# Streaming-encoder layer with a 32-expert MoE on one core: weight streaming in 2 MB buffers with 16 KB pieces

## The chip, the cores and the metric

One core of one Trainium2 chip runs the whole layer, as one program. The metric is the device time in microseconds; a version's time is the median of its runs. Three runs of the kernel before took 1102.35, 1105.44 and 1106.4 us.

## The reference

Input x is 1 x 256 x 1024 in float32. One layer is computed: LayerNorm; a mixer (differential attention with 4 heads beside a gated recurrent branch, both from one 1024 x 2560 projection, then a 1024 x 1024 output projection); a residual LayerNorm; a mixture of experts; a last residual LayerNorm. The mixture is where the bytes are:

```
logits = xt @ w_router + b_router          # 256 tokens, 32 experts
top_v, top_e = lax.top_k(logits, 4);  gates = softmax(top_v)
h = xb @ w_gu[e] + b_gu[e]                 # w_gu[e]: 1024 x 2048
x_glu = minimum(h[..., ::2], 7);  x_lin = clip(h[..., 1::2], -7, 7)
y = (x_glu * sigmoid(1.702 * x_glu) * (x_lin + 1)) @ w_down[e] + b_down[e]   # 1024 x 1024
out = sum over a token's experts of gate * y
```

All weights are float32. An expert has 8 MB of w_gu and 4 MB of w_down, so 32 experts are 384 MB, and every one of them is read once from HBM.

## The kernel before

The mixer comes first. Its weights (w_in in five blocks of 512 columns, w_out in two of 512 rows) and then the experts' weights pass through 1 MB buffers of 8 KB per partition. `wtile` takes one from a pool: pool 0 (`wpool`) has NW1 = 12 buffers in rotation; nine further pools of one buffer each (`wpool2`) are opened only when the mixer's tiles have been given back (L852, ahead of the main loop), in the memory that those tiles had. That makes 21. `SLOTS` says which pool each of 21 successive transfers takes.

`load_chunk` issues the next transfer of `seq`, which lists (expert, h). For h below 8 it is 128 neighbouring rows of w_gu, one row of 8 KB per partition, so a transfer consists of 128 pieces of 8 KB. For h = 8 to 11 it is 256 rows of w_down, two neighbouring rows per partition, also 8 KB. All are issued by SP's queue, in program order. Each transfer takes one of eight completion semaphores in turn and waits until the transfer eight before it has landed; it also waits until TensorE has done the last matmul on the buffer's old content (`reuse_waits="tile"`: on the tile as a whole). `NPRE` = 7 expert transfers are issued while the mixer runs, the other 14 of the first 21 where the nine pools open, and from then on `ahead(e, h)` issues as many as keep the program 21 transfers in front of what expert e has used.

The main loop goes over the experts. `first(e)` runs `gu_mm`: for each of the 8 row blocks k of w_gu four accumulating matmuls per half (two halves b), 64 token slots (CAP) against 512 columns, in the order k = 0 to 5 with both halves, then k = 6 and 7 for each half; then SwiGLU on DVE and ACT. After it come the combine of the pair before, the transposes of the activations (`act_t`), the gather of the next pair's tokens (`gather_mm`) and `down_mm` with the four w_down buffers in four steps. An expert with more than 64 tokens first runs `overflow(e)`, the same work for the surplus, on the same weight buffers. The last two experts' w_gu transfers go ahead of their w_down transfers.

One further transfer group stands in `seq` in front of the w_down of expert LATE = 13: b_down and two LayerNorm rows, three small DMAs into a buffer of the stream, which `start_acc` reads at expert 13.

Features: with one row per partition, row block k holds features 128k to 128k+127. Every operand that is multiplied with w_gu or scaled per feature (`rows_t`, `gather_ps`, `gb1`, the router weights `wr`) has that order.

Of the kernel before, what the change touches and what calls it, by code (L numbers as in the profile page):

```python
# [9 lines left out]
F32 = mybir.dt.float32  # L10
# [7 lines left out]
P = 128  # L18
D = 1024
T = 256  # L20
NT = T // P
KT = D // P
H = 4
NE = 32
# [6 lines left out]
BIGGEST = 3.4028234663852886e38  # L31
NW1 = 12
NW2 = 7
NW3 = 2
LATE = 13
NPRE = 7
SLOTS = (0, 0, 0, 0, 0, 0, 0, 3, 0, 1, 2, 4, 0, 0, 6, 0, 0, 7, 5, 8, 9)
NH = 12
NOF = (T - CAP) // OCAP
# [10 lines left out]
def trunk(ctx, tc, x, ln0_g, ln0_b, w_in, conv_w, conv_b, w_rg_a, b_rg_a, w_rg_x, b_rg_x,  # L50
# [37 lines left out]
    def wtile(name, pool=0):  # L88
        return (wpool, *wpool2)[pool].tile([P, 2048], F32, tag=f"w{pool}", name=name)

    def load_in(c, parts=1, between=()):

        src = w_in[0][:, c * 512:(c + 1) * 512].rearrange("(j p) n -> p j n", p=P)
        ws = []
        for h in range(2):
            w = wtile(f"win{c}_{h}").rearrange("p (j n) -> p j n", j=4)
            n = 4 // parts
            for i in range(0, 4, n):
                SP.dma_start(w[:, i:i + n], src[:, 4 * h + i:4 * h + i + n])
            ws.append(w)  # L100
            for dst, src_s in between if h == 0 else ():
                SP.dma_start(dst, src_s)
        return ws

    def load_out(c):
        ws = []
        for h in range(2):
            w = wtile(f"wout{c}_{h}").rearrange("p (j n) -> p j n", j=2)
            o = c * 512 + h * 256
            SP.dma_start(w, w_out[0][o:o + 256, :].rearrange("(j p) n -> p j n", p=P))  # L110
            ws.append(w)
        return ws
# [47 lines left out]
    wr = pb.tile([P, KT, NE], F32, name="wr")  # L160
    SP.dma_start(wr, w_router[0].rearrange("(j p) e -> p j e", p=P))
    br = pb.tile([1, NE], F32, name="br")
# [12 lines left out]

    seq = [(e, h) for e in range(NE - 2) for h in range(NH)]
    seq += [(NE - 2 + i // KT, i % KT) for i in range(2 * KT)]
    seq += [(e, h) for e in (NE - 2, NE - 1) for h in range(KT, NH)]
    seq.insert(LATE * NH + KT, (LATE, NH))

    def load_chunk():


        i = nchunk[0]
        nchunk[0] += 1
        e, h = seq[i]
        w = wtile(f"we{e}_{h}", SLOTS[i % len(SLOTS)])
        if h < KT:
            SP.dma_start(w, w_gu[0, e][h * P:(h + 1) * P, :])
        elif h == NH:  # L190
            SP.dma_start(w[:NE, :D], b_down[0])
            SP.dma_start(w[NE:NE + 1, :D], ln1_b)
            SP.dma_start(w[:1, D:], ln1_g)
        else:
            s = w_down[0, e].rearrange("(g b p j) n -> p g b (j n)", g=2, p=P, j=2)[:, (h - KT) % 2, (h - KT) // 2]

            for g in (slice(0, D), slice(D, 2 * D)) if i == len(seq) - 1 else (slice(0, 2 * D),):
                SP.dma_start(w[:, g], s[:, g])
        W[e, h] = w

# [53 lines left out]
    def bcast_row(ps, rows, j, start=True, stop=True):  # L254

        PE.matmul(ps, ident[:16, j:j + 1].to_broadcast([16, P]), rows, start=start, stop=stop, skip_group_check=True)

    def small_transpose(dst, src, ps, rows):
# [312 lines left out]
    V.tensor_scalar(gsub, gsub, 1.0 - LAM_INIT, None, op0=OP.mult)  # L571
    small_transpose(gb1.rearrange("p r k -> p (r k)"), rows_1, ps1("gb1_ps"), 16)

# [128 lines left out]
    def rows_t(t, n):  # L702
        ps = ps2(f"rT{t}_{n}")[:, 0] if t == 0 else ps1(f"rT{t}_{n}")
        for j in range(4):
            k = n * 4 + j
            PE.transpose(ps[:, j * P:(j + 1) * P], acc[t][:, k * P:(k + 1) * P], ident)
        return A.activation(rT[:, n * 4:n * 4 + 4, t * P:(t + 1) * P], ps.rearrange("p (j n) -> p j n", j=4), AF.Copy)
# [78 lines left out]
    def gather_ps(S, ps, k, t, start):  # L786
        n = S.shape[-1]
        PE.matmul(ps[:, (k % 4) * n:(k % 4 + 1) * n], n1[t][:, k * P:(k + 1) * P], S[:, t],  # L788
                  start=start, stop=t == NT - 1, skip_group_check=True)
# [61 lines left out]
    sa.close()  # L851
    for i in range(NW2 + NW3):  # L852
        wpool2.append(ctx.enter_context(tc.tile_pool(name=f"wpool{i + 2}", bufs=1, reuse_waits="tile")))
    for _ in range(NW1 - NPRE + NW2 + NW3):
        load_chunk()
    s1p.close()
    pdn = loop.enter_context(tc.tile_pool(name="pdn", bufs=1, space=PSUM, reuse_waits="tile", side="right"))
# [166 lines left out]
    def start_acc(n):  # L1024

        w = W[LATE, NH]
        ns = slice(n * 512, (n + 1) * 512)
# [25 lines left out]
    def ahead(e, h):  # L1053

        while nchunk[0] < min(len(seq), NH * e + h + (e > LATE or (e == LATE and h == NH)) + len(SLOTS)):
            load_chunk()

    def first(e, mid=None):
        gi, gj = where[e]
        ps = gu_mm(e, xgs[gi][1], gj * CAP, CAP, mid)  # L1060
        ahead(e, KT)
        g = gtile(e)
        for b in range(2):
            swiglu(e, ps, b, g)
        return g
# [143 lines left out]
```

## Time and profile before

| | |
|---|---|
| median of three runs | 1105.44 us |
| the profiled execution | 1104.07 us, span 1102.4 us |
| mean granted TensorE clock | 0.974 |
| TensorE busy | 1015.0 us, 92% |
| VectorE / ScalarE / GpSimd busy | 281.0 / 188.6 / 146.6 us |
| read from HBM | 420.52 MB, 382 GB/s over the span |
| w_gu | 256 transfers of 1024 KB, median 20.8 us from issue to landing |
| w_down | 127 of 1024 KB and 2 of 512 KB, median 19.8 us |

The page cuts the span into 40 slices of 27.6 us. TensorE is busy for most of every slice, and so are the DMA engines, so that neither share alone tells which of them the end waits for. That has to be read from what TensorE waits for, stretch by stretch.

### The profile page before, as it was taken

Reading aid. Unit: us, or ns where it says so; the run is one execution under the profiler, and the core shown is the slowest. Engines: PE = TensorE matmul, PEld = TensorE weight load, DVE = VectorE, ACT = ScalarE, POOL = GpSimd, SP = SyncE. Lnnn points to the kernel's source line nnn. Section 1 sums busy time; section 2 is a strip of 40 time slices with the busy share of each in tenths; the row PEclk is TensorE's granted clock in tenths of the full one; section 3 lists DMA queues with packets and bytes.
Section 4 is the critical chain, followed back from the end, with each engine's and each line's share of the span. In section 5 each row is a group of like instructions: output and inputs, shape, how many; then the busy total and the mean of one; then the engine's idle time right before and its main releaser. Section 6 shows DMA issues by size and latency. Waiting matters only on the chain. (4 is left out here: it accounts for less than half of the span.)

```text
span 1102.4 us, 12947 instructions
## 1 busy us (share of the span) xinstructions
PE 1015.0 (92%) x4942; PEld 466.1 (42%) x4942; DVE 281.0 (25%) x625; ACT 188.6 (17%) x426; POOL 146.6 (13%) x221
## 2 busy tenths in 40 slices
PE   8999999999899989888999898988888889999895
PEld 8987644444344433333343333333333434444331
DVE  7978311122022201214211011212111122221023
ACT  5675211111011101110011011110100101111011
POOL 4583202010101010101001010101001001010001
PEclk9999999999999999998899999999999989999998
DMA  8987799999999999989999999999999999999962
GB/s 276 323 335 306 293 393 420 418 419 419 419 419 419 419 419 419 405 352 395 421 419 418 420 410 404 411 393 401 415 389 414 418 391 420 387 410 396 409 272 81
DMA packets 66139, 423.46 MB, mean 384 GB/s; under 512 B 8925, under 2 KB 8990, under 8 KB 16960
## 3 DMA queue, kind: packets, MB, share of 16 engines
q1 hardware_dynamic: 65984, 421.60, 94.5%
q8 instruction: 72, 1.18, 0.4%
q14 instruction: 83, 0.68, 0.2%
HBM read 420.52 MB, written 1.05 MB: 382 GB/s over the span
## 5 line engine op out<-in xcount | busy, mean ns | idle before, releaser
L878 PE MATMUL h<-we,xg 128*64 128x512 f32 (+1 forms) x2112 | 481.8, 610 | 58.9 <-DMA we<-in_w_gu_dram 44.6
L878 PEld LDWEIGHTS h<-we,xg 128*64 128x64 f32 (+1 forms) x2112 | 160.8, 138 | 375.6 <-issue 306.4
L911 PE MATMUL y<-we,actT 128*64 128x512 f32 x1024 | 228.9, 599 | 0.1
L888 DVE TENSOR_SCALAR g<-h 128x256 f32<-128x256 f32 x65 | 27.6, 425 | 694.6 <-PE h L878 694.6
L926 POOL TENSOR_SCALAR sgate<-iota,posm,gate 128x64 f32<-128x64 f32 x96 | 54.1, 582 | 814.9 <-PE gt_ps L934 813.9
L889 ACT ACTIVATE sg<-g 128x256 f32<-128x256 f32 x65 | 27.0, 416 | 596.6 <-DVE g L888 596.6
L911 PEld LDWEIGHTS y<-we,actT 128*64 128x64 f32 x1024 | 71.3, 137 | 135.1 <-issue 128.6
L788 PE MATMUL xg_ps<-S,n 128*128 128x128 f32 (+1 forms) x544 | 67.4, 278 | 0.0
L788 PEld LDWEIGHTS xg_ps<-S,n 128*128 128x128 f32 x544 | 66.3, 195 | 2.6 <-issue 1.6
L940 PE MATMUL cb<-ysb,gtT 128*128 128x512 f32 x116 | 57.5, 618 | 0.0
L1103 ACT ACTIVATE ysb<-y 128x512 f32<-128x512 f32 x30 | 16.3, 595 | 139.2 <-PE y L911 139.2
L942 DVE TENSOR_TENSOR acc<-acc,cb 128x512 f32<-128x512 f32 x58 | 39.5, 681 | 0.0
L385 PE MATMUL pj<-xo,hi 128*128 128x256 f32 x128 | 37.0, 289 | 1.0 <-DVE xo L340 1.0
L796 DVE TENSOR_SCALAR xg<-xg_ps,gb 128x128 f32<-128x128 f32 (+1 forms) x68 | 22.8, 398 | 59.1 <-PE xg_ps L788 59.1
L385 PE MATMUL pj<-xh,hi 128*128 128x256 f32 x128 | 37.2, 291 | 0.2 <-ACT xh L334 0.2
L899 PE MATMUL actT_ps<-ident,g 128*128 128x128 f32 x130 | 29.9, 312 | 7.3 <-DVE g L892 6.3
L385 PE MATMUL pj<-xh,lo 128*128 128x256 f32 x128 | 36.4, 284 | 0.0
L940 PEld LDWEIGHTS cb<-ysb,gtT 128*128 128x128 f32 x116 | 19.6, 189 | 37.9 <-ACT sg L889 21.1
L252 POOL TENSOR_TENSOR lo<-win,hi 128x1024 fp32r<-128x1024 f32 x11 | 32.7, 2993 | 13.0 <-PE pj L385 12.9
L899 PEld LDWEIGHTS actT_ps<-ident,g 128*128 128x128 f32 x130 | 21.6, 202 | 25.0 <-DVE g L892 12.3
L798 ACT ACTIVATE xg<-xg_ps,gb 128x128 f32<-128x128 f32 (+1 forms) x68 | 25.3, 452 | 31.8 <-PE xg_ps L788 31.8
L670 PE MATMUL h<-bgu,pick 128*128 128x512 f32 x64 | 30.5, 479 | 0.0
(271 smaller groups left out, 701.1 us busy)
## 6 DMA issues: line engine op xcount, KB each, us to landing
we<-in_w_gu_dram SPq DMA_DIRECT2D x256, 1024.0 KB, 20.8
we<-in_w_down_dram SPq DMA_DIRECT2D x127, 1024.0 KB, 19.8
win<-in_w_in_dram SPq DMA_DIRECT2D x8, 1024.0 KB, 10.9
wout<-in_w_out_dram SPq DMA_DIRECT2D x4, 1024.0 KB
win<-in_w_in_dram SPq DMA_DIRECT2D x4, 512.0 KB, 8.9
x<-in_x_dram SPq DMA_DIRECT2D x4, 256.0 KB, 3.1
we<-in_w_down_dram SPq DMA_DIRECT2D x2, 512.0 KB
out_dram<-acc SPq DMA_DIRECT2D x4, 256.0 KB, 2.3
```

The lines of the kernel that those rows point to most:

```text
L252: return (eng or V).tensor_sub(lo, src, f32(hi))
L385: PE.matmul(ps[m // 2][:, m % 2], a, b, start=k == 0 and m % 2 == 0 and i == 0, stop=k == KT - 1 and i == 2, skip_group_check=True)
L670: PE.matmul(ps[b], picks[e].rearrange("p g w -> p (g w)"), bgs[b], start=True, stop=False, skip_group_check=True)
L788: PE.matmul(ps[:, (k % 4) * n:(k % 4 + 1) * n], n1[t][:, k * P:(k + 1) * P], S[:, t], start=start, stop=t == NT - 1, skip_group_check=True)
L878: PE.matmul(ps[b][g * w:(g + 1) * w], xg[k // 4][:, k % 4, o:o + w], W[e, k][:, c0:c0 + 512], start=False, stop=k == KT - 1, skip_group_ch ...
L888: V.tensor_scalar(g[:, ns], ps[b][:, 0::2], 7.0, None, op0=OP.min)
L889: A.activation(s, g[:, ns], AF.Sigmoid, scale=1.702)
L899: PE.transpose(ps[:, j * P:(j + 1) * P], gj[:, j], ident)
L911: PE.matmul(ps[n][gs], at[:, 2 * b + j, g * CAP:(g + 1) * CAP], w_dn(e, 2 * g + b, j, n * 512, 512), start=c + j == 0, stop=c + j == 4, sk ...
L926: G.tensor_scalar(sg[:, t, i * CAP:(i + 1) * CAP], iota2[:, 0], posm[:, t, o:o + 1], gate[:, t, o:o + 1], op0=OP.is_equal, op1=OP.mult)
L940: PE.matmul(pp, gt[:, n, t * P:(t + 1) * P], y, start=True, stop=True)
L942: V.tensor_add(acc[t][:, ns], acc[t][:, ns], pp)
```

## The change

Buffers become 2 MB, 16 KB per partition: six in pool 0 and four pools of one, ten in all, plus one 1 MB buffer `bd` that holds b_down and the two rows for good. A w_gu transfer is 256 neighbouring rows, two per partition, as 128 pieces of 16 KB; four of them make an expert. A w_down buffer is filled by two transfers of 1 MB, whose pieces stay 8 KB. w_in and w_out keep their 1 MB transfers, two of which now share a buffer. The three small DMAs move from expert 13 to the place where the pools open. Features are paired to match (feature 2p + j of a 256 block in partition p, row block j), so transposes and gathers read every second column, `gb1` is built by four small matmuls in the place of one, and `wr` is loaded in pieces of 256 bytes where it was 128.

```diff
-NW1 = 12
-NW2 = 7
-NW3 = 2
+NW1 = 6
-NPRE = 7
-SLOTS = (0, 0, 0, 0, 0, 0, 0, 3, 0, 1, 2, 4, 0, 0, 6, 0, 0, 7, 5, 8, 9)
-NH = 12
+NPRE = 4
+SLOTS = (0, 0, 0, 0, 2, 1, 0, 4, 0, 5)
+NH = 6
+NU = 4
...
-        return (wpool, *wpool2)[pool].tile([P, 2048], F32, tag=f"w{pool}", name=name)
+        return (wpool, *wpool2)[pool].tile([P, 4096], F32, tag=f"w{pool}", name=name)
...
-    seq.insert(LATE * NH + KT, (LATE, NH))
...
-        if h < KT:
-            SP.dma_start(w, w_gu[0, e][h * P:(h + 1) * P, :])
-        elif h == NH:
-            SP.dma_start(w[:NE, :D], b_down[0])
-            SP.dma_start(w[NE:NE + 1, :D], ln1_b)
-            SP.dma_start(w[:1, D:], ln1_g)
...
+        if h < NU:
+            SP.dma_start(w, w_gu[0, e].rearrange("(d p j) n -> p d (j n)", p=P, j=2)[:, h])
+            for j in range(2):
+                W[e, 2 * h + j] = w[:, j * 2 * D:(j + 1) * 2 * D]
+            return
+        for g in range(2):
+            s = w_down[0, e].rearrange("(g b p j) n -> p g b (j n)", g=2, p=P, j=2)[:, g, h - NU]
+            c = KT + 2 * (h - NU) + g
+            W[e, c] = w[:, g * 2 * D:(g + 1) * 2 * D]
...
+                SP.dma_start(W[e, c][:, q], s[:, q])
...
+    def pairs(ap):
+
+        return ap.rearrange("p (d q j) -> p d j q", q=P, j=2)
...
-            PE.transpose(ps[:, j * P:(j + 1) * P], acc[t][:, k * P:(k + 1) * P], ident)
+            PE.transpose(ps[:, j * P:(j + 1) * P], pairs(acc[t])[:, k // 2, k % 2], ident)
...
-        PE.matmul(ps[:, (k % 4) * n:(k % 4 + 1) * n], n1[t][:, k * P:(k + 1) * P], S[:, t],
+        PE.matmul(ps[:, (k % 4) * n:(k % 4 + 1) * n], pairs(n1[t])[:, k // 2, k % 2], S[:, t],
...
-    for _ in range(NW1 - NPRE + NW2 + NW3):
+        if i == 2:
+            bd = wpool2[2].tile([P, 2 * D], F32, name="bd")
+    for _ in range(len(SLOTS) - NPRE):
         load_chunk()
+    SP.dma_start(bd[:NE, :D], b_down[0])
+    SP.dma_start(bd[NE:NE + 1, :D], ln1_b)
+    SP.dma_start(bd[:1, D:], ln1_g)
...
-        while nchunk[0] < min(len(seq), NH * e + h + (e > LATE or (e == LATE and h == NH)) + len(SLOTS)):
+        while nchunk[0] < min(len(seq), NH * e + h + len(SLOTS)):
...
-        ahead(e, KT)
+        ahead(e, NU)
```

Where it moves instructions: on SP's queue alone (of the other engines' orders only one copy at expert 13 changes place, and `gb1`'s small matmuls are more). First the queue at the end of the first 20 or 21 MB. `weE_H` is transfer H of expert E; DMAHW0 to DMAHW7 are the eight completion semaphores, the other names are the engines whose use of the memory is waited for. Before, the rows from expert 1's fifth w_gu transfer on:

```order
L189 DMA we1_4_1483<-in_w_gu_dram 128x2048 [waits DMAHW0_49,DVE_49]
L189 DMA we1_5_1485<-in_w_gu_dram 128x2048 [waits DMAHW1_49,PE_49]
L189 DMA we1_6_1487<-in_w_gu_dram 128x2048 [waits DMAHW2_49,PE_49]
L189 DMA we1_7_1489<-in_w_gu_dram 128x2048 [waits DMAHW3_49]
L198 DMA we1_8_1491<-in_w_down_dram 128x2048 [waits DMAHW4_49]
L997 UNCONDITIONAL_BRANCH
L198 DMA we1_9_2528<-in_w_down_dram 128x2048 [waits DMAHW5_49,PE_49]
L198 DMA we1_10_2530<-in_w_down_dram 128x2048 [waits DMAHW6_49,PE_49]
L198 DMA we1_11_2532<-in_w_down_dram 128x2048 [waits DMAHW7_49,PE_49]
L189 DMA we2_0_2534<-in_w_gu_dram 128x2048 [waits DMAHW0_49,PE_49]
```

The same place of the changed kernel:

```order
L189 DMA we1_2_1454<-in_w_gu_dram 128x4096 [waits DMAHW2_49,DVE_49,Pool_49]
L189 DMA we1_3_1456<-in_w_gu_dram 128x4096 [waits DMAHW3_49,PE_49]
L867 DMA bd_1437<-in_b_down_dram 32x1024 [waits DMAHW4_49,PE_49]
L868 DMA bd_1437<-in_ln1_b_dram 1x1024 [waits DMAHW5_49]
L869 DMA bd_1437<-in_ln1_g_dram 1x1024 [waits DMAHW6_49]
L1011 UNCONDITIONAL_BRANCH
L199 DMA we1_4_2496<-in_w_down_dram 128x2048 [waits DMAHW7_49,PE_49]
L199 DMA we1_4_2496<-in_w_down_dram 128x2048 [waits DMAHW0_49]
L199 DMA we1_5_2499<-in_w_down_dram 128x2048 [waits DMAHW1_49,PE_49]
L199 DMA we1_5_2499<-in_w_down_dram 128x2048 [waits DMAHW2_49]
L189 DMA we2_0_2502<-in_w_gu_dram 128x4096 [waits DMAHW3_49,PE_49]
```

The branch stands where the first 21 transfers (one of them expert 1's first w_down) or the first 20 MB are out; the three small DMAs stand ahead of it now. Behind it each buffer waits for TensorE's use of expert 0's weights, once per 1 MB before and once per 2 MB now.

Second, expert 13. Before:

```order
L189 DMA we13_6_14648<-in_w_gu_dram 128x2048 [waits DMAHW2_49,PE_49]
L189 DMA we13_7_14650<-in_w_gu_dram 128x2048 [waits DMAHW3_49,PE_49]
L191 DMA we13_12_14652<-in_b_down_dram 32x1024 [waits DMAHW4_49,PE_49]
L192 DMA we13_12_14652<-in_ln1_b_dram 1x1024 [waits DMAHW5_49]
L193 DMA we13_12_14652<-in_ln1_g_dram 1x1024 [waits DMAHW6_49]
L198 DMA we13_8_15652<-in_w_down_dram 128x2048 [waits DMAHW7_49,PE_49]
```

Now:

```order
L189 DMA we13_2_14498<-in_w_gu_dram 128x4096 [waits DMAHW5_49,PE_49]
L189 DMA we13_3_14500<-in_w_gu_dram 128x4096 [waits DMAHW6_49,PE_49]
L199 DMA we13_4_15498<-in_w_down_dram 128x2048 [waits DMAHW7_49,PE_49]
L199 DMA we13_4_15498<-in_w_down_dram 128x2048 [waits DMAHW0_49]
L199 DMA we13_5_15501<-in_w_down_dram 128x2048 [waits DMAHW1_49,PE_49]
```

The three small DMAs, which each took one of the eight semaphores, are gone from the stream; eight transfers in flight are 8 MB before and 12 MB now, four of 2 MB and four of 1 MB.

## Rows read from the trace of the kernel before

**Rows 1.** The page: TensorE's busy time, and GB/s in 40 slices.

```profile
PE 1015.0 (92%) x4942; PEld 466.1 (42%) x4942; DVE 281.0 (25%) x625; ACT 188.6 (17%) x426; POOL 146.6 (13%) x221
...
GB/s 276 323 335 306 293 393 420 418 419 419 419 419 419 419 419 419 405 352 395 421 419 418 420 410 404 411 393 401 415 389 414 418 391 420 387 410 396 409 272 81
```

**Rows 2.** Waits of TensorE, 390 to 881 us: total us, times, longest.

```profile
PE h L878 <- DMA we<-in_w_gu_dram: 44.0, 59, 1.7
```

**Rows 3.** The same view from 881.5 us to the end.

```profile
PE h L878 <- issue: 3.0, 1, 3.0
...
PE h L878 <- DMA we<-in_w_gu_dram: 0.6, 1, 0.6
```

**Rows 4.** TensorE's timeline, experts 12 and 13: start, us, group [idle before].

```profile
469.53 1.94 PE L878 MATMUL h<-we,xg 128*64 128x512 f32 x8 [0.54 <-DMA we<-in_w_gu_dram]
472.03 1.08 PE L878 MATMUL h<-we,xg 128*64 128x512 f32 x4 [0.56 <-DMA we<-in_w_gu_dram]
474.52 2.79 PE L878 MATMUL h<-we,xg 128*64 128x512 f32 x12 [1.41 <-DMA we<-in_w_gu_dram]
...
503.36 1.08 PE L878 MATMUL h<-we,xg 128*64 128x512 f32 x4 [0.60 <-DMA we<-in_w_gu_dram]
506.16 4.29 PE L878 MATMUL h<-we,xg 128*64 128x512 f32 x12 [1.72 <-DMA we<-in_w_gu_dram]
```

**Rows 5.** TensorE's timeline, expert 24's end and expert 25's overflow.

```profile
851.22 2.80 PE L878 MATMUL h<-we,xg 128*64 128x512 f32 x12 [1.40 <-DMA we<-in_w_gu_dram]
...
878.56 1.94 PE L878 MATMUL h<-we,xg 128*32 128x512 f32 x8 [1.41 <-DMA we<-in_w_gu_dram]
881.05 1.94 PE L878 MATMUL h<-we,xg 128*32 128x512 f32 x8 [0.56 <-DMA we<-in_w_gu_dram]
...
897.43 13.95 PE L878 MATMUL h<-we,xg 128*64 128x512 f32 x64 [0.45 <-PEq L1003]
```

**Rows 6.** Stretches: length, busy time of each engine, clock, DMA share, GB/s.

```profile
30.00:35.00 5.00, 5.00 (x45) 5.00 (x44) 5.00 (x6) 2.12 (x2) 3.27 (x2) 1.00 1.04 390
210.00:240.00 30.00, 29.79 (x146) 12.91 (x144) 5.66 (x14) 3.37 (x8) 4.99 (x10) 1.00 1.01 419
480.00:510.00 30.00, 25.41 (x114) 8.63 (x112) 1.71 (x5) 2.50 (x7) 0.00 (x0) 0.94 0.85 335
```

**Rows 7.** Waits of SP's queue: total us, times, longest.

```profile
SPq L198 <- DMA we<-in_w_gu_dram: 240.3, 108, 3.1
...
SPq L189 <- PE y L911: 31.1, 17, 8.3
```

**Rows 8.** TensorE's timeline, experts 0 and 1.

```profile
125.17 5.37 PE L878 MATMUL h<-we,xg 128*64 128x512 f32 x24 [0.30 <-PEq L997]
...
132.46 8.80 PE L878 MATMUL h<-we,xg 128*64 128x512 f32 x40
...
148.05 7.09 PE L911 MATMUL y<-we,actT 128*64 128x512 f32 x32
155.29 13.95 PE L878 MATMUL h<-we,xg 128*64 128x512 f32 x64 [0.16 <-PEq L997]
```

**Rows 9.** SP's timeline from 127 us (first) and from 141 us (second).

```profile
127.14 0.33 SPq L198 DMA_DIRECT2D we<-in_w_down_dram  x1
...
141.30 9.05 SPq L189 DMA_DIRECT2D we<-in_w_gu_dram  x2
```

**Rows 10.** The page's DMA queues (packets, MB, share of 16 engines) and issues.

```profile
q1 hardware_dynamic: 65984, 421.60, 94.5%
q8 instruction: 72, 1.18, 0.4%
...
we<-in_w_gu_dram SPq DMA_DIRECT2D x256, 1024.0 KB, 20.8
```

**Rows 11.** The page's groups: weight loads from adjacent and from every second column.

```profile
L788 PEld LDWEIGHTS xg_ps<-S,n 128*128 128x128 f32 x544 | 66.3, 195 | 2.6 <-issue 1.6
...
L899 PEld LDWEIGHTS actT_ps<-ident,g 128*128 128x128 f32 x130 | 21.6, 202 | 25.0 <-DVE g L892 12.3
```

More of the change, by code (lines that the diff above doesn't have):

```diff
@@ L94, in load_in @@
         ws = []
+        ww = wtile(f"win{c}").rearrange("p (h j n) -> p h j n", h=2, j=4)
         for h in range(2):
-            w = wtile(f"win{c}_{h}").rearrange("p (j n) -> p j n", j=4)
+            w = ww[:, h]
             n = 4 // parts
@@ L106, in load_out @@
         ws = []
+        ww = wtile(f"wout{c}").rearrange("p (h j n) -> p h j n", h=2, j=2)
         for h in range(2):
-            w = wtile(f"wout{c}_{h}").rearrange("p (j n) -> p j n", j=2)
+            w = ww[:, h]
             o = c * 512 + h * 256
@@ L160, in trunk @@
     wr = pb.tile([P, KT, NE], F32, name="wr")
-    SP.dma_start(wr, w_router[0].rearrange("(j p) e -> p j e", p=P))
+    SP.dma_start(wr.rearrange("p (d j) e -> p d (j e)", j=2), w_router[0].rearrange("(d p j) e -> p d (j e)", p=P, j=2))
     br = pb.tile([1, NE], F32, name="br")
@@ L176, in trunk @@
     seq = [(e, h) for e in range(NE - 2) for h in range(NH)]
-    seq += [(NE - 2 + i // KT, i % KT) for i in range(2 * KT)]
-    seq += [(e, h) for e in (NE - 2, NE - 1) for h in range(KT, NH)]
-    seq.insert(LATE * NH + KT, (LATE, NH))
+    seq += [(NE - 2 + i // NU, i % NU) for i in range(2 * NU)]
+    seq += [(e, h) for e in (NE - 2, NE - 1) for h in range(NU, NH)]
     def load_chunk():
@@ L187, in load_chunk @@
         w = wtile(f"we{e}_{h}", SLOTS[i % len(SLOTS)])
-        if h < KT:
-            SP.dma_start(w, w_gu[0, e][h * P:(h + 1) * P, :])
-        elif h == NH:
-            SP.dma_start(w[:NE, :D], b_down[0])
-            SP.dma_start(w[NE:NE + 1, :D], ln1_b)
-            SP.dma_start(w[:1, D:], ln1_g)
[L194 to L199, printed above, removed]
+        if h < NU:
[7 more added lines that the diff above has]
+            W[e, c] = w[:, g * 2 * D:(g + 1) * 2 * D]
+            for q in (slice(0, D), slice(D, 2 * D)) if (i, g) == (len(seq) - 1, 1) else (slice(0, 2 * D),):
+                SP.dma_start(W[e, c][:, q], s[:, q])
     def w_dn(e, m, j, c0, n):
@@ L571, in trunk @@
     V.tensor_scalar(gsub, gsub, 1.0 - LAM_INIT, None, op0=OP.mult)
-    small_transpose(gb1.rearrange("p r k -> p (r k)"), rows_1, ps1("gb1_ps"), 16)
+    ps = ps1("gb1_ps")
+    for j in range(2):
+        for h in range(2):
+            PE.matmul(ps[h * 64:(h + 1) * 64, 8 * j:8 * j + 8], rows_1.rearrange("r (q j) -> r j q", j=2)[:, j],
+                      ident[:16, :16].rearrange("r (d h) -> r h d", h=2)[:, h], start=True, stop=True)
+    V.tensor_copy(gb1.rearrange("p r (d j) -> p j (r d)", j=2), ps[:, :16].rearrange("p (j q) -> p j q", j=2))
     on = unit("U2", "on", (P, NT, H, P))
@@ L851, in trunk @@
     sa.close()
-    for i in range(NW2 + NW3):
+    for i in range(5):
         wpool2.append(ctx.enter_context(tc.tile_pool(name=f"wpool{i + 2}", bufs=1, reuse_waits="tile")))
-    for _ in range(NW1 - NPRE + NW2 + NW3):
+        if i == 2:
+            bd = wpool2[2].tile([P, 2 * D], F32, name="bd")
+    for _ in range(len(SLOTS) - NPRE):
         load_chunk()
+    SP.dma_start(bd[:NE, :D], b_down[0])
+    SP.dma_start(bd[NE:NE + 1, :D], ln1_b)
+    SP.dma_start(bd[:1, D:], ln1_g)
     s1p.close()
@@ L1024, in start_acc @@
     def start_acc(n):
-        w = W[LATE, NH]
+        w = bd
         ns = slice(n * 512, (n + 1) * 512)
```

## The prediction

> **What bounds the kernel now.** I read the page first: TensorE is busy for 92% of the span and the DMA engines move about 419 GB/s through the middle of it [rows 1]. Shares of two engines that are both nearly full decide nothing, so I went on to what TensorE waits for, by stretch. Between 390 and 881 us it waits 44.0 us, in 59 waits, all for a w_gu transfer [rows 2]. After 881.5 us it waits 0.6 us for one [rows 3]. So the stream paces the kernel up to 881 us, and TensorE's own work (with 3.0 us of unexplained issue time) fills the last 221 us.
>
> The timeline shows the pacing. In expert 12 groups of eight or twelve matmuls, each on one newly landed megabyte, start at 469.53, 472.03 and 474.52: one landing per 2.49 us [rows 4]. The place where the stream lets go is expert 25, whose surplus tokens are worked off first: 1.94 us for row block 6 from 878.56, then the last wait, for row block 7, which ends at 881.05 [rows 5]. While TensorE is busy with the surplus until 897.43, the stream gets ahead, and it is not caught again.
>
> The long pace is a little slower than 2.49: the same step (the last twelve matmuls) stands at 474.52 in expert 12 and at 851.22 in expert 24 [rows 4, 5], 376.7 us for 144 MB, or 2.616 us per MB. A transfer has landed when the slowest of 16 engines has done its share, so this is not the page's GB/s. The hole between 480 and 510 us proves it: 335 GB/s in the place of 419 [rows 6], where three small DMAs hold three of the eight completion semaphores, while the steps on the far side still stand 2.80 us apart (503.36 and 506.16) against 2.49 [rows 4]. The mean rate lost 6 us there; the path lost 0.3 us.
>
> So one microsecond saved per stream position counts only ahead of expert 25's last w_gu transfer. What the stream saves behind that is hidden by TensorE's work.
>
> **The pieces of 16 KB.** The time of one piece is share x 16 engines x bytes / rate. From 30 to 35 us only w_in's 2 KB pieces run: 1.04 x 16 x 2048 / 390 = 87.4 ns. From 210 to 240 us it is 8 KB pieces: 1.01 x 16 x 8192 / 419 = 315.9 ns [rows 6]. The difference is 76.2 ns per 2 KB, which leaves 11.2 ns fixed per piece. A 16 KB piece would then take 11.2 + 8 x 76.2 = 620.8 ns in the place of 631.8. Each engine has 8 such pieces in a 2 MB transfer, so a transfer saves 8 x 11.2 = 90 ns. Experts 3 to 25 have 23 x 4 = 92 transfers between the start of the unbroken stream and its last binding landing: **-8.2 us**. Bounds: nothing, if a 16 KB piece is worth two of 8 KB; and at most 16 us, if all that the pace of 2.616 has over pure bytes (8 x 4 x 76.2 ns = 2.44 us per MB) belonged to pieces and were halved for 184 MB of w_gu. I take the middle, which is the one that two rows measure.
>
> The Trainium skill, "DMA: Bandwidth & Descriptors", section "Why small descriptors are slow (HBM only)", puts the overhead at some 3 cycles per packet against one cycle per 32 bytes, and calls joining descriptors worthwhile up to 256 bytes only; that speaks against this change. By it the fixed part of an 8 KB piece would be 3/259 of 316 ns, an estimate of 3.7 ns, the saving 2.7 us, and the whole sum +3.0 us. The rows show three times that fixed part, so I stay with them.
>
> **The start of the stream.** SP's first issue that waits for expert 0's weights is at 127.14 [rows 9], when 21 MB are out. TensorE's groups of 8 matmuls per row block then free 1 MB about every 1.8 us, faster than the 2.5 us that a megabyte takes, until w_gu is used up: 29 MB are out by 141.6. The next buffer is a w_down buffer, free after a quarter of `down_mm` (148.05 + 1.8), and SP issues at 150.03, the end of the second row of [rows 9] less the issue itself. In the changed kernel, 20 MB are out; the first 2 MB come free after row block 1 (125.17 + 3.6 = 128.8 [rows 8]), the fourth buffer at the end of w_gu (132.46 + 8.8 = 141.3), so 28 MB are out and moved by about 128.8 + 8 x 2.5 = 148.8. The next buffer is half of w_down and comes free at 148.05 + 3.5 = 151.6. At 151.6 the old stream has 29 + 1.6 / 2.5 = 29.6 MB, the new one 28: it starts 1.6 MB behind, **+4.1 us**. Further buffers come in time: the second half of w_down is free at 155.1 and needed at 156.6, expert 1's first pair of row blocks at 155.29 + 3.5 = 158.8 and needed at 161.6. Bounds 2 us (part of the old stream's idle time is latency that both pay) to 7 us (one more 2 MB release of 3.5 us is late).
>
> **The last landing.** Row blocks 6 and 7 now land together. TensorE has both still to do when expert 25's last transfer arrives, 2 x 1.94 us in the place of 1.94 [rows 5]: **+1.9 us**; at the other clock level half of it. In the earlier experts the same costs nothing: the next transfer is later still.
>
> **The three small DMAs.** Away from the stream at expert 13 they give back the 0.3 us above: **-0.3 us**. Ahead of the branch they stand behind transfers which end before the first release, in the gap just worked out: nothing, and if that gap closes, the same 0.3 us.
>
> **Edits at nothing.** Weight loads from every second column: the activation transposes do that already, at 202 ns against 195 [rows 11]. 7 ns x 544 is 3.8 us in all, hidden by waits up to 881 us; behind it six experts x 16 loads x 7 ns = 0.7 us at most. Three more small matmuls for `gb1`: under 0.5 us. `wr` in larger pieces, shared buffers for w_in and w_out: they are issued and landed long before their readers, and what SP waits for most is landings, 240.3 us in the largest group against 31.1 us in the largest one for TensorE [rows 7]. Semaphore waits removed from SP and TensorE: their queues wait for landings anyway.
>
> **The sum:** -8.2 + 4.1 + 1.9 - 0.3 = -2.5 us. The profiled execution took 1104.07 us, so 1101.6; the median of the three runs is 1.37 us above it, and by it I predict **1102.9 us**. About 0.5% (5.5 us) is what a measurement of this kernel can tell from no change.
>
> **Rivals.**
> - The pieces gain nothing, because the queue cuts 16 KB in two or the fixed part hangs on bytes: the change doesn't do what it says. For: only 2 and 8 KB are seen in quantity. Against: the two windows of [rows 6]. Time 1102.9 + 8.2 = 1111.1, or with a third of the fixed part 1108. Chance 0.13.
> - The pieces gain the upper bound, near 16 us: 1095. For: the pace holds 0.18 us per MB more than bytes. Against: instruction fetches share the engines and keep their part. Chance 0.13.
> - The hole at expert 13 is on the path after all: -6.0 us in the place of -0.3, 1097.2. Against: the steps in [rows 4]. Chance 0.10.
> - Slower: buffers come free too late. A 2 MB buffer waits for both its row blocks, up to 1.8 us more than before, and 20 MB are in front of TensorE, not 21. From the point where SP's queue of eight runs empty before the buffer is free, the stream has a hole per expert. Place: experts 2 to 9, where TensorE is behind the stream and SP waits up to 8.3 us for it [rows 7]. Price: 8 x 1.8 = 14 us, 1117. Against: 20.8 us from issue to landing [rows 10], and 419 GB/s without a hole there [rows 6]. Chance 0.09.
> - Slower: a 16 KB piece is dear. The 16.4 KB packets of the instruction queue take 0.004 x 16 x 1102.4 / 72 = 0.98 us each [rows 10], not 0.62. At that price a transfer costs 8 x 0.35 = 2.8 us more, 128 of them 360 us: about 1460 us. They go elsewhere than a buffer's rows, though, and seldom follow each other. Chance 0.03.
> - Slower: TensorE's instruction fetches queue behind longer pieces. TensorE lost 3.0 us to issue in the last stretch [rows 3]; with 72 fetches each 0.3 us later, 23 us if all were exposed, 1126. The Trainium skill (same page, "Queues, rings and completion order") says that an engine drains a whole packet before it turns to another ring. Nearly all fetches are hidden now. Chance 0.03.
>
> **Chances and range.** My forecast keeps 0.49. Faster by over 0.5% (below 1099.9): the two gains, 0.23, and a fifth of the forecast's own spread: 0.33. Slower (above 1111.0): half of "nothing gained", the three slow rivals: 0.21, less a little as gains may coincide with them: 0.18. The same: 0.49. The range takes in the two gains and the case without one: 1094 to 1111.5; left out are the three slow rivals and the edges.
>
> **What would show it.** Steps of two row blocks, 16 matmuls after each wait, 4.9 us apart and not 4.98; about 49,600 packets; TensorE's waits for w_gu below 44 us in sum and none behind expert 25; expert 25's last wait ending at 876 to 878 us, and the time from there to the end unchanged but for the 1.9 us. Issue at 151 to 152 us with a gap before it confirms the start. I am wrong if the pace per 12 MB is not 0.3 to 0.4 us under the old 31.4, or if TensorE waits for w_gu after 900 us.

## The result and the profile after

Over the same rounds the changed kernel took 1098.93 us (median of 7 runs, 1098.42 to 1101.56) and the kernel before 1105.44 us (7 runs, 1102.21 to 1107.93). The ratio is 0.995, with a 95% interval of 0.9931 to 0.9969: 6.5 us (0.6%) faster by the medians and 5.5 us by the ratio, at the edge of the 0.5% that can be told from no change. The forecast was 1102.9, 4 us too high, inside its range. The profiled execution took 1100.57 us with a span of 1098.9, that is 3.5 us less than the one before.

The page of the changed kernel, against [rows 1] and [rows 10]: TensorE's and the other engines' busy time, GB/s in 40 slices, and the largest DMA queue.

```profile
PE 1008.3 (92%) x4948; PEld 472.8 (43%) x4948; DVE 277.8 (25%) x625; ACT 188.7 (17%) x426; POOL 146.6 (13%) x221
...
GB/s 268 334 247 318 293 377 426 422 423 423 423 423 423 422 423 423 422 425 426 423 424 420 410 423 412 420 410 394 415 395 411 423 198 424 425 425 422 424 292 82
...
q1 hardware_dynamic: 47040, 421.59, 92.9%
```

The middle of the stream runs at 423 GB/s in the place of 419, and the DMA engines move the same bytes in 92.9% of a shorter span instead of 94.5%. The slice with 198 stands at 880 us: there the buffers are full, and SP waits up to 19.9 us for TensorE's use of a buffer, which costs nothing.

TensorE's waits for w_gu from 390 to 881 us, against the 44.0 us of [rows 2]:

```profile
PE h L892 <- DMA we<-in_w_gu_dram: 46.9, 36, 2.4
```

And its largest waits from 881.5 us to the end, against [rows 3]:

```profile
PE actT_ps L913 <- DVE g L906: 3.2, 1, 3.2
PE h L892 <- PEq L1011: 0.9, 5, 0.2
```

The first view is as forecast in kind (fewer and longer waits, one per 2 MB), though its sum went up, not down. The second holds the surprise by what it lacks: the 3.0 us of "issue" of [rows 3] have no answer in the changed kernel.

TensorE's timeline in experts 12, 13, 24 and 25, against [rows 4] and [rows 5]:

```profile
477.83 3.65 PE L892 MATMUL h<-we,xg 128*64 128x512 f32 x16 [1.27 <-DMA we<-in_w_gu_dram]
...
498.42 3.65 PE L892 MATMUL h<-we,xg 128*64 128x512 f32 x16 [1.25 <-DMA we<-in_w_gu_dram]
503.35 3.65 PE L892 MATMUL h<-we,xg 128*64 128x512 f32 x16 [1.27 <-DMA we<-in_w_gu_dram]
508.25 3.65 PE L892 MATMUL h<-we,xg 128*64 128x512 f32 x16 [1.25 <-DMA we<-in_w_gu_dram]
...
850.26 3.65 PE L892 MATMUL h<-we,xg 128*64 128x512 f32 x16 [1.06 <-DMA we<-in_w_gu_dram]
...
879.85 3.50 PE L892 MATMUL h<-we,xg 128*32 128x512 f32 x16 [2.40 <-DMA we<-in_w_gu_dram]
...
896.83 15.58 PE L892 MATMUL h<-we,xg 128*64 128x512 f32 x64 [0.45 <-PEq L1017]
```

Two row blocks land every 4.9 us (4.93 and 4.90), as forecast. From expert 12's last step to expert 24's it is 372.43 us; before it was 376.7. Expert 25's last wait ends at 879.85 against 881.05, and TensorE takes up expert 25 proper at 896.83 against 897.43. So the stream and all that stands ahead of it won 0.6 us in this pair of profiles. From there to the end of the span are 202.07 us against 204.97: **2.9 of the 3.5 us were won where TensorE's own work sets the end**, and where the prediction had moved nothing.

### The profile page after: what moved, and what is told of

The parts are those of the page before. It is cut to its first block, busy times and chain, and to the rows that moved or that the text cites. A ratio compares the mean times of both kernels' runs of the same rounds, so it can differ in the third digit from the quotient of the medians.

```text
span 1098.9 us, 12603 instructions
## 1 busy us (share of the span) xinstructions
PE 1008.3 (92%) x4948; PEld 472.8 (43%) x4948; DVE 277.8 (25%) x625; ACT 188.7 (17%) x426; POOL 146.6 (13%) x221
## 3 DMA queue, kind: packets, MB, share of 16 engines
q1 hardware_dynamic: 47040, 421.59, 92.9%
## 5 line engine op out<-in xcount | busy, mean ns | idle before, releaser
L892 PE MATMUL h<-we,xg 128*64 128x512 f32 (+1 forms) x2112 | 469.8, 603 | 63.1 <-DMA we<-in_w_gu_dram 50.6
L797 PE MATMUL xg_ps<-S,n 128*128 128x128 f32 (+1 forms) x544 | 70.5, 284 | 0.0
L797 PEld LDWEIGHTS xg_ps<-S,n 128*128 128x128 f32 x544 | 69.5, 199 | 2.5 <-issue 1.6
L252 POOL TENSOR_TENSOR lo<-win,hi 128x1024 fp32r<-128x1024 f32 x11 | 32.9, 3014 | 12.3 <-PE pj L389 12.2
```

Of the source, the lines that this page charges most:

```text
L252: return (eng or V).tensor_sub(lo, src, f32(hi))
L797: PE.matmul(ps[:, (k % 4) * n:(k % 4 + 1) * n], pairs(n1[t])[:, k // 2, k % 2], S[:, t], start=start, stop=t == NT - 1, skip_group_check=True)
L892: PE.matmul(ps[b][g * w:(g + 1) * w], xg[k // 4][:, k % 4, o:o + w], W[e, k][:, c0:c0 + 512], start=False, stop=k == KT - 1, skip_group_ch ...
```

## The experiments

The theories: 1, the account of the prediction, in which pieces of 16 KB win, the start of the stream loses, and behind expert 25 nothing changes; 2, fewer and larger transfers win, pieces don't; 3, the gain is what befalls TensorE behind 881 us. Theory 4 came later, from the profiles.

### Pieces of 8 KB in 2 MB transfers

The changed kernel with this edit, and without the pairing of features (`wr`, `gb1` and `pairs` as they were):

```diff
-            SP.dma_start(w, w_gu[0, e].rearrange("(d p j) n -> p d (j n)", p=P, j=2)[:, h])
+            SP.dma_start(w.rearrange("p (j n) -> p j n", j=2), w_gu[0, e].rearrange("(d j p) n -> p d j n", p=P, j=2)[:, h])
```

> The changed kernel with pieces of 8 KB in its w_gu transfers (two pieces per partition from rows 128 apart, features in their old order); buffers, 2 MB transfers, the moved small DMAs and all waits stay. Theory 1: the saving of the pieces goes, 80 to 90 ns for each of 92 transfers, 7.4 to 8.3 us: 1106 to 1107.5 against 1099, w_gu's landings 4.97 us apart again, expert 25's last wait at 887 to 888. Theory 2 (larger and fewer transfers, or the hole at expert 13, bring the gain; the pieces nothing): within 1.5 us of the changed kernel, 1098 to 1100.5. Theory 3: 1097 to 1101, since the stretch behind expert 25 does not depend on the pieces.

Measured: 1105.55 us (12 runs), against 1098.99 for the changed kernel over the same rounds: +6.6 us. Theory 2 falls, and theory 1's size is a little high. TensorE's timeline of this kernel, the same steps as above:

```profile
481.40 3.65 PE L887 MATMUL h<-we,xg 128*64 128x512 f32 x16 [1.31 <-DMA we<-in_w_gu_dram]
...
502.14 3.65 PE L887 MATMUL h<-we,xg 128*64 128x512 f32 x16 [1.29 <-DMA we<-in_w_gu_dram]
507.12 3.65 PE L887 MATMUL h<-we,xg 128*64 128x512 f32 x16 [1.33 <-DMA we<-in_w_gu_dram]
...
856.68 3.65 PE L887 MATMUL h<-we,xg 128*64 128x512 f32 x16 [1.32 <-DMA we<-in_w_gu_dram]
```

The landings are 4.98 us apart again, and from 481.40 to 856.68 it is 375.28 us: 2.85 more than with 16 KB over 12 experts, or 59 ns for each of 48 transfers. Over 92 transfers that is 5.5 us. Against the kernel before (376.7) this kernel is 1.4 us shorter between the same steps, though its pieces are the same; it has no hole at expert 13 (the run with the small DMAs back prices that).

### The pairing alone

The kernel before with `pairs` in the transposes and gathers, `gb1` and `wr` as in the change, and 1 MB transfers of every second row:

```diff
-            SP.dma_start(w, w_gu[0, e][h * P:(h + 1) * P, :])
+            SP.dma_start(w, w_gu[0, e].rearrange("(d p j) n -> p d j n", p=P, j=2)[:, h // 2, h % 2])
```

> The kernel before with the pairing of features alone: transposes and gathers read every second column, gb1 by four small matmuls, wr in 256-byte pieces, and a 1 MB w_gu transfer takes every second row (pieces of 8 KB as before, 16 KB apart). Buffers, transfers and waits are those of the kernel before. Theory 1: the pairing is worth nothing, 1105 to 1106; with the run that has 8 KB pieces and no pairing, the 6.6 us between it and the changed kernel then belong to the 16 KB pieces alone. Rival (half of that is the pairing, by another order of rows in HBM): 1101 to 1103.

Measured: 1105.53 us (12 runs), ratio to the kernel before 1.0 (0.9988 to 1.0012). The pairing is worth nothing, and the 6.6 us above belong to the pieces.

### The small DMAs back at expert 13

```diff
+        if (e, h) == (LATE, NU):
+            bd = late[0]
+            SP.dma_start(bd[:NE, :D], b_down[0])
+            SP.dma_start(bd[NE:NE + 1, :D], ln1_b)
+            SP.dma_start(bd[:1, D:], ln1_g)
```

> The changed kernel with the three small DMAs back at expert 13, ahead of its w_down, into the same buffer of their own. Theory 1: the hole of the stream returns in the GB/s between 480 and 510 us, but the landings close up, so the path loses 0 to 1 us: 1099 to 1100. Its rival (the hole was on the path and gave the gain): +5 to +6 us, 1104 to 1105.

Measured: 1099.52 us (12 runs), +0.5 us by the medians; by the ratios to the kernel before (0.9958 against 0.9946) +1.3. This stretch of its profile answers to [rows 6]:

```profile
480.00:510.00 30.00, 25.13 (x121) 9.56 (x119) 3.06 (x7) 2.99 (x9) 0.00 (x0) 1.00 0.84 322
```

The hole is back: 322 GB/s in the place of 423, or 30 x (1 - 322 / 423) = 7 us of transfer time. About 1 us of it reaches the end. The forecast's 0.3 was low, and the rival with 6 is out.

### The start of the stream

One step of TensorE moved in the changed kernel: the gather for experts 2 and 3 goes behind expert 0's `down_mm`.

```diff
-        need(where[e][0] + 1, G, where[e][1])
+        if e > 0:
+            need(where[e][0] + 1, G, where[e][1])
...
                 down_mm(e, at, ps, j)
             ahead(e, NH)
+            if e == 0:
+                need(1, G, 0)
```

> The changed kernel with one step of TensorE moved: the gather of the next pair's tokens (16 matmuls, 3.0 us), which stands ahead of expert 0's down_mm, goes behind it. Nothing is left out. It frees expert 0's first w_down buffer, on which the stream stands at 28 MB, some 2 to 3 us earlier. Theory 1 (a microsecond at the start of the stream is a microsecond at the end): 2 to 2.7 us faster than the changed kernel, 1096.3 to 1097; 32 MB landed 2 to 2.7 us earlier, expert 25's last wait likewise. Rival (the start does not bind, since TensorE catches up with the stream later anyway, or the next buffer is late instead): within 0.8 us of 1099.

Measured: 1099.03 us (6 runs), so no gain over 1098.99. SP's timeline of the changed kernel shows the waits in question (its first two groups in the stretch from 126.8 to 152.9 us, the others behind it):

```profile
130.74 6.48 SPq L199 DMA_DIRECT2D we<-in_w_down_dram  x4
139.85 3.76 SPq L189 DMA_DIRECT2D we<-in_w_gu_dram  x2
...
153.68 3.76 SPq L189 DMA_DIRECT2D we<-in_w_gu_dram  x2
160.91 4.24 SPq L199 DMA_DIRECT2D we<-in_w_down_dram  x4
```

And the same of the kernel with the step moved:

```profile
139.81 10.93 SPq L189 DMA_DIRECT2D we<-in_w_gu_dram  x3
...
159.73 4.54 SPq L199 DMA_DIRECT2D we<-in_w_down_dram  x4
```

The issue that waits for expert 0's first w_down buffer went from 153.68 to 150.41 (139.81 + 10.93 less one issue of 0.33), but the one behind it, which waits for expert 1's first two row blocks, only from 160.91 to 159.73. The next buffer is late instead; the rival's second half was right. Of 3.3 us won at one release, 1.2 were left at the next.

### The same two kernels again

Unchanged copies, for more profiles: the kernel before three times, the changed kernel once.

> The kernel before, unchanged, for a second profile. Theory 1 (account: 16 KB pieces speed the stream by about 7.5 us up to expert 25's last w_gu, the start gives about 6 of it back, behind expert 25 TensorE's own work is the bound): the last w_gu wait of expert 25 ends at 881 us within 1 us again, and what differs between executions lies behind it, as issue time and as half-clock stretches of TensorE. Theory 3 (the rest of the gain is what befalls TensorE behind 881 us): the 3.0 us of issue near 1031 us comes again, or another of 1.5 us or more in the last 220 us. If the stretch from 881 us to the end is free of issue time this time and the total is still 1104 to 1106, theory 3 falls.

> The changed kernel, unchanged, for a second profile. Theory 1: the last w_gu wait of expert 25 ends at 880 us within 1 us, w_gu lands every 4.89 us in expert 12; total 1097 to 1101. Theory 3: no issue time of TensorE over 1 us in the last 220 us, so that the end is 3 us or more shorter than in the kernel before beyond what the start of expert 25's rest explains.

> The kernel before, unchanged, for a third profile. Two profiled executions (1104.07 and 1101.28) lie below the median of 31 plain ones (1105.1). Theory 1: expert 25's last wait ends at 880 to 882 us again; an execution of 1105 or more shows the excess as issue time, half-clock stretches or waits for w_gu behind it. Theory 3: issue time of TensorE of 1.5 us or more behind 881 us.

> As the third profile of the kernel before. If three of four profiled executions have less than 1.1 us of issue time behind 881 us, such stalls are not what the kernel before loses on average; if the last wait of expert 25 ends later than 883 us in one of them, the stream's own spread is.

Measured: 1104.67 us (12 runs; its profiled execution 1101.28), 1098.99 (8 runs; profiled 1097.86), and single executions of 1103.62 and 1106.09. Expert 25's last wait ended between 880.33 and 882.36 in the four profiles of the kernel before. In all four TensorE has issue time in the same place behind it, of 3.00, 1.01, 1.64 and 2.44 us; in the changed kernel's two profiles there is none there. TensorE's timeline of the kernel before, first profile, at expert 6 (its group is shown up to 300 us), expert 19 and expert 30:

```profile
290.57 9.64 PE L878 MATMUL h<-we,xg 128*64 128x512 f32 x36 [2.79 <-issue]
683.33 13.72 PE L878 MATMUL h<-we,xg 128*64 128x512 f32 x53 [2.27 <-issue]
...
1028.79 1.94 PE L878 MATMUL h<-we,xg 128*64 128x512 f32 x8 [0.19 <-PEq L997]
1033.72 13.99 PE L878 MATMUL h<-we,xg 128*64 128x512 f32 x56 [3.00 <-issue]
```

Expert 30's 64 matmuls take 18.92 us from 1028.79 to 1047.71. In the changed kernel they take 13.95:

```profile
1030.25 13.95 PE L892 MATMUL h<-we,xg 128*64 128x512 f32 x64 [0.19 <-PEq L1011]
```

The loss is 5.0 us, not 3.0, as the stretches of the kernel before tell:

```profile
1031.00:1033.50 2.50, 0.00 (x0) 0.00 (x0) 0.00 (x0) 0.00 (x0) 0.00 (x0) 1.00 1.01 406
1035.00:1038.00 3.00, 3.00 (x10) 0.88 (x8) 0.00 (x0) 0.00 (x0) 0.00 (x0) 0.50 1.00 410
1040.00:1047.00 7.00, 7.00 (x34) 2.41 (x32) 0.93 (x3) 0.42 (x1) 0.00 (x0) 1.00 1.01 396
```

TensorE did nothing for 3 us, and shortly after the granted clock is 0.50, that is 1.2 GHz: 10 matmuls in 3 us where 7 us at 2.4 GHz hold 34. In the second and third profile the clock did not fall after shorter stalls; in the fourth, with a stall of 2.44 us, it did:

```profile
1031.47 1.94 PE L878 MATMUL h<-we,xg 128*64 128x512 f32 x8 [0.18 <-PEq L997]
1035.85 13.87 PE L878 MATMUL h<-we,xg 128*64 128x512 f32 x56 [2.44 <-issue]
```

The changed kernel has three such stalls too, at experts 5, 15 and 24:

```profile
267.00 11.38 PE L892 MATMUL h<-we,xg 128*64 128x512 f32 x52 [2.59 <-issue]
567.89 0.59 PE L892 MATMUL h<-we,xg 128*64 128x512 f32 x1 [1.94 <-issue]
...
840.34 8.86 PE L892 MATMUL h<-we,xg 128*64 128x512 f32 x38 [1.56 <-issue]
```

Its third one stands ahead of expert 25, where TensorE catches up with the stream and waits for w_gu again (the row at 850.26 above): it is paid by a wait that would have been there. The places belong to the version, not to the execution: 8 KB pieces in 2 MB transfers have them at 267.16, 571.80 and 845.25 (the last of 0.47 us), and the pairing with 1 MB transfers at 290.44, 683.78 and 1034.26. So theory 3 holds for a part of the gain, and theory 4 asks why the places moved: each stall stands 8 to 12 matmuls behind the jump over an expert's overflow code.

The Trainium skill, "Runtime: NRT & Kernel Launch", section "Instruction fetch mechanics", says that an engine's instructions are fetched ahead in blocks, strictly in sequence, and that a taken branch to a place outside the blocks at hand makes the engine wait for a fetch. By that, the stall comes wherever a block ends shortly behind the jump, and instructions that are never executed would move it. The runs that follow agree, except that the stall comes 8 to 12 matmuls behind the jump and not at it.

The traces show the fetch itself. The queue of instructions with packets of 16.4 KB (q8 in [rows 10]) has 72 or 73 packets in a whole execution. That is one in some 15 us; yet each of the 38 stalls of this kind (issue time of over 1 us in `gu_mm`) in the 14 profiles ends 2.28 to 2.79 us, once 3.37, after one of them began. At expert 30 in the four profiles of the kernel before the packet began at 1031.25, 1030.02, 1032.35 and 1033.56, and TensorE went on 2.47, 2.61, 2.63 and 2.29 us later. So the stall is long or short by how early its packet begins.

### Moving the stalls by code that is never executed

Both kernels with more matmuls in expert 0's overflow branch for more than 160 tokens, which no expert has here. None of them is executed (TensorE's records have one semaphore instruction more, and no matmul). The number is 55 for the kernel before and 67 for the changed one:

```diff
                     for i in range(3, NOF):
                         more(e, i)
+                    if e == 0:
+                        pad = mc("pad")
+                        for i in range(55):
+                            PE.matmul(pad[:, :P], ident, ident, start=True, stop=True)
```

> The kernel before with 55 matmuls more in a branch of expert 0 that is never taken (over 160 tokens for one expert). Nothing is left out and nothing more is executed; TensorE's program behind that place is only some 110 instructions further on. Theory 4 (TensorE's issue time is a fetch of instructions that is late behind the jump over an expert's overflow code, whenever a block of the program ends just there; in five profiles with 1 MB buffers it stands at experts 6, 18 and 29, in five with 2 MB buffers at experts 5, 15 and 24): the three places move by about five experts, none lies behind 882 us any more, the time from expert 25's first matmul behind its overflow to the end falls from 204.4 to some 201.6 us, and the median by 2 to 3 us, to 1102.3 to 1103.5. Rival (the stall belongs to what is done at expert 29, or to transfers of 1 MB): issue time of 1 to 3 us near 1031 us stays, and the median within 1 us of 1105.3.

> The changed kernel with 67 matmuls more in the same branch of expert 0 that is never taken: some 134 instructions. Theory 4: the places at experts 5, 15 and 24 move by about five experts, so that one falls at expert 28 to 30, behind 882 us, where TensorE sets the end: issue time of 1 to 3 us there and the median 1.5 to 3 us up, 1100.5 to 1102. Rival (with 2 MB buffers there is no such stall in the last stretch): no issue time behind 882 us, 1099 within 1 us.

Measured: 1105.34 us (12 runs) and 1099.96 us (12 runs); neither went as expected. The stalls of the first of them:

```profile
238.84 13.99 PE L878 MATMUL h<-we,xg 128*64 128x512 f32 x56 [3.19 <-issue]
621.82 13.72 PE L878 MATMUL h<-we,xg 128*64 128x512 f32 x53 [2.29 <-issue]
982.71 13.99 PE L878 MATMUL h<-we,xg 128*64 128x512 f32 x56 [2.12 <-issue]
```

And of the second:

```profile
264.41 12.29 PE L892 MATMUL h<-we,xg 128*64 128x512 f32 x56 [2.82 <-issue]
565.70 12.30 PE L892 MATMUL h<-we,xg 128*64 128x512 f32 x56 [2.46 <-issue]
```

They moved, so they hang on the layout and not on what an expert does, but by another amount: two experts ahead in the first (to 4, 17 and 28, the last one still exposed), and by 3 or 4 matmuls in the second, whose third stall is not seen any more and whose time is at the edge of its rival's 1 us. The two amounts settle the block. A float32 `PE.matmul` of the kernel is four instructions, two weight loads and two multiplications: the nine matmuls of just this form that the kernel executes at its start (`busy(WARM)`, L302) leave 18 of each.

```profile
L302 PE MATMUL lnb<-ident 128*128 128x128 f32 x18 | 4.2, 430 | 3.3 <-POOL ident masks.py:199 3.3
L302 PEld LDWEIGHTS lnb<-ident 128*128 128x128 f32 x18 | 3.9, 330 | 3.3 <-POOL ident masks.py:199 3.3
```

So 55 and 67 of them are 220 and 268 instructions, twice the 110 and 134 of the expectations, and that is why five experts was wrong. With blocks of 256 instructions 220 is 36 short of a block and 268 is 12 over one. The spacing of the stalls (about 12 experts before, 9.5 now) makes 21 and 27 instructions of drift per expert: 36 is two experts of drift, 12 a few matmuls. (The next two expectations count two instructions for a dead matmul, and so have blocks of 128; all their numbers of instructions are half of the true ones, and the places that follow are the same. The expectation above calls the second and third place before "18 and 29"; counted by groups they are 19 and 30.) With that rule two numbers were chosen again, 25 for the kernel before and 33 for the changed one.

> The kernel before with 25 matmuls more in the branch of expert 0 that is never taken; nothing is left out and nothing more is executed. 55 matmuls moved the three stalls two experts ahead, 67 in the changed kernel moved them by 4 matmuls only. Both fit a block of 128 instructions (110 is 18 short of a block, 134 is 6 over one; 9 to 13 instructions of drift per expert). Theory 4 with that block: 50 instructions move the places by 4 to 5 experts, so that two are left, near experts 10 or 11 and 22 or 23, and none behind 882 us; the time from expert 25's first matmul behind its overflow to the end is 201.5 to 202.5 us, where profiles with the stall have 203 to 206, and the median falls by 2 to 3 us, to 1102.3 to 1103.3. Rival (the places move, but another takes the third one's place, or the median does not follow): issue time of 1 us or more behind 882 us, or a median within 1 us of 1105.2.

> The changed kernel with 33 matmuls more in the same branch of expert 0 that is never taken. Theory 4 with blocks of 128 instructions: 66 instructions move the places at experts 5, 15 and 24 by five, so that one stands at experts 28 to 30, behind 882 us: issue time of 1 to 3 us there, the time from expert 25's first matmul to the end 203 to 205 us in the place of 202.1, and the median 1.5 to 3 us up, 1100.5 to 1102. Rival (with 2 MB buffers the last stretch has no such stall whatever the layout): no issue time behind 882 us and 1099 within 1 us.

Measured: the kernel before with 25 dead matmuls took **1100.84 us** (5 runs, 1100.5 to 1102.48; ratio to the kernel before 0.9956, 0.9943 to 0.997), the changed kernel with 33 took **1104.73 us** (11 runs, 1102.59 to 1106.34; ratio 0.9989, 0.9979 to 0.9999). The one won 5 us by code that never runs (4.9 by the ratio, 5.2 by the medians); the other lost 4.3 to 5.8 against the changed kernel (ratios of 0.995 and 0.9946 in its two sets of runs; the most by the medians). The stalls of the first, and its expert 30:

```profile
401.82 11.21 PE L878 MATMUL h<-we,xg 128*64 128x512 f32 x44 [2.79 <-issue]
810.79 0.59 PE L878 MATMUL h<-we,xg 128*64 128x512 f32 x1 [1.17 <-issue]
...
1032.17 13.95 PE L878 MATMUL h<-we,xg 128*64 128x512 f32 x64 [0.19 <-PEq L997]
```

Two are left, at experts 10 and 23, four further on than before (the third would be at 34, which doesn't exist), and expert 30 takes 13.95 us. The second kernel:

```profile
405.44 13.93 PE L892 MATMUL h<-we,xg 128*64 128x512 f32 x54 [2.26 <-issue]
715.18 9.22 PE L892 MATMUL h<-we,xg 128*64 128x512 f32 x38 [1.95 <-issue]
...
1004.50 2.79 PE L892 MATMUL h<-we,xg 128*64 128x512 f32 x12 [0.16 <-PEq L1011]
1010.43 12.94 PE L892 MATMUL h<-we,xg 128*64 128x512 f32 x52 [3.13 <-issue]
```

Experts 10, 20 and 29, each five further on, as the rule said, and expert 29 takes 18.87 us. Only the size was expected too small. In the profiles the exposed stall costs 1.3 to 5.0 us, by its length and by whether the clock falls behind it; in the medians about 5. The four profiles of the kernel before take 204.97, 202.98, 203.60 and 205.98 us from expert 25's first matmul behind its overflow to the end, the one with 25 dead matmuls 201.68: 2.7 us less than their mean, about half of what the medians say. The plain executions have no trace, so where the other half goes is open.

Compared with like layouts, the change is worth 1.9 us without an exposed stall (1098.93 against 1100.84), but these medians come from different rounds; by the ratios to the kernel before (0.995 and 0.9946 against 0.9956) it is 0.7 to 1.1 us. With a stall in both it is 1.2 us (ratio 0.9989 of the changed kernel with 33 dead matmuls, 0.1 to 2.3 us by its interval). None of these is far from no change.

The run with 8 KB pieces has no exposed stall either, and against the kernel before with 25 dead matmuls (1105.55 and 1100.84, ratios 1.0001 and 0.9956) it prices the rest of the change: 2 MB buffers without the larger pieces lose 4.7 to 5.0 us, and the pieces win 6.1 to 6.6.

## Why the prediction was right or wrong

| term | forecast | measured |
|---|---|---|
| pieces of 16 KB | -8.2 us | -5.5 (step from expert 12 to 24), -6.6 (medians) |
| start of the stream | +4.1 us | +6.1 in the first pair, 4.2 of it behind expert 0's start |
| last landing | +1.9 us | +1.6 in the first pair |
| three small DMAs | -0.3 us | -0.5 to -1.3 |
| sum of these | -2.5 us | -0.7 to -1.9 (like layouts, by ratios and medians) |
| waits taken out of TensorE's queue, as "edits at nothing" | 0 | about -5 (-4.9 by moving the stall in the kernel before), by the place of a stall |

**What bounds the kernel** was read rightly: the stream up to expert 25, TensorE behind it. (The 0.6 us for w_gu in [rows 3] are not a wait behind 881.5 us; they are the 0.56 us ahead of 881.05 in [rows 5], whose group reaches into that view.) A stall of TensorE behind expert 25 counts in full; one ahead of it was paid by waits for w_gu that follow, as at 850.26 in the changed kernel.

**The pieces** were right in mechanism and too large in size: 59 ns for a transfer of 2 MB in the trace, where 90 ns had come from two rows of [rows 6]. The pace fell by 0.355 us per 12 MB (376.69 against 372.43 us over 144 MB), inside the 0.3 to 0.4 that was asked for, but partly by luck: 0.12 of it came with 2 MB transfers of 8 KB pieces too (375.28), so that the pieces made 0.24. The price of 2 KB pieces in the mixer was a far neighbour to work from. By the Trainium skill's rule in "DMA: Bandwidth & Descriptors", section "Why small descriptors are slow (HBM only)", 2.7 us was the estimate; the measurement lies between it and the forecast, at about twice the rule.

**The start**: the working held where it could be followed. The 2 MB behind expert 0's w_down were to be issued once half of `down_mm` was done, 3.5 us behind its start; TensorE's `down_mm` began at 149.98 and SP issued at 153.68. Before, the thirtieth megabyte was issued at 150.03 [rows 9]; now the 29th and 30th at 153.68, which is 3.65 us and one megabyte of 2.49: 6.1 us. 1.9 of it is that TensorE began expert 0 at 127.06 and not at 125.17 [rows 8]. In other profiles it began between 124.12 and 125.66 before and between 124.82 and 128.01 with 2 MB buffers, so a part of that is the execution's own spread, and how large a part is open. How much of the delay reaches the end is seen in sum only: the start, the last landing and the three small DMAs together were forecast at +5.7 and cost 4.7 to 5.0 by the comparison of like layouts above.

**The last landing** cost its two row blocks: 3.50 us behind the wait in the place of 1.94, at the lower clock. In the second profile of the changed kernel the same 16 matmuls took 1.92, as the prediction's other end had it.

**The step that failed** is in the paragraph on edits at nothing: "Semaphore waits removed from SP and TensorE: their queues wait for landings anyway." As time they are nothing. As instructions they are a part of the program's layout, and the layout decided at which expert a fetch is late. The 3.0 us of issue in [rows 3] were read and then left standing in both kernels, as if they belonged to TensorE's work in the last 221 us. That the pieces and the pairing do not move the stalls is shown by the two runs above. The traces say which instructions do. The run with 8 KB pieces executes the 4942 matmuls and 4942 weight loads of the kernel before, but 186 semaphore instructions of TensorE in the place of 223 (35 of the 37 are missing in `gu_mm`), and has its stalls at the new places; the run with the pairing executes 4948, 4948 and 223, and has them at the old ones. So among the instructions that leave a record it is the waits, and the change does not touch SP's queue alone: TensorE's program is shorter by them. The code that is skipped leaves none, and the waits were not put back alone.

The time lies in the range because the range is 17.5 us wide. Most of the gain comes from a term that the sum had at nothing, so the 4 us between forecast and result do not speak for the sum; the like layouts do.

**The rivals.** Of those with less gain or a loss none came about: SP's waits for `down_mm` grew (66.4 us in 15, the longest 10.0, against 31.1 in [rows 7]), but the stream had no hole in the middle, and 16 KB pieces were not dear. The rival on instruction fetches named the right engine and the right event with the wrong sign: it feared longer waits for each fetch, where the number of exposed stalls went from one to none. Forecasts that held: 16 matmuls per wait, 4.9 us apart, no wait for w_gu behind expert 25. The packets were forecast at 49,600 and were 47,040: besides the pieces, 128 fewer transfers make 2048 less, 16 for each (63936 against 65984 in the run with 8 KB pieces), and `wr` in larger pieces makes 512 less (65472 in the run with the pairing). Missed as well: the sum of waits below 44 us, and the last wait at 876 to 878 us, since the start lost more and the pieces won less.

## What to carry to other kernels

Where a page shows an engine idle with no releaser on the stretch that sets the end, price it as a term that any edit of that engine's program can move, and look at whether it stands at the same instruction in every execution. Before a change of half a per cent is believed, run the old and the new kernel in more than one layout of the program: here dead code alone moved either kernel by some 5 us, more than twice what the change itself was worth in like layouts. A place for such a stall is ahead of the last wait for a slower resource, where it is paid by waiting.

## What was not expected of the hardware

TensorE's stalls follow blocks of 256 instructions: 220 dead instructions moved them two experts ahead, 268 by a few matmuls, 100 by four experts and 132 by five. The Trainium skill, "Runtime: NRT & Kernel Launch", section "Instruction fetch mechanics", gives 256 instructions as a block and calls the crossing mostly hidden. The block is as it says; the crossing behind a jump cost 1.0 to 3.1 us where it was exposed, or up to 5 with what followed. Stalls of 2.12 to 3.13 us in the last stretch were followed by 56 or 52 matmuls with a part at the clock of 0.50 (four profiles); after stalls of 1.01, 1.64 and 2.00 us 56 matmuls took 12.3 us, without it (three profiles). The length of the stall alone does not decide: at expert 6 of the run with the pairing 56 matmuls took 12.29 us after a stall of 2.90 us.

A hole of 30 us at 322 GB/s in the DMA stream cost the end 0.5 to 1.3 us and not the 7 that the mean rate lost: the landings close up again behind it.
